# Nine weight blocks of the merge multiplied as seven products of quarters instead of eight

## The chip, the cores and the metric

One core of a Trainium2 chip runs the whole program. The metric is the time of one execution on the device in microseconds (us); the kernel before has a median of 2540.18 us over 3 runs (2537.29 to 2540.43). The core has a matrix engine (TensorE, PE in the profile, with its weight loads as PEld), a vector engine (DVE), a scalar engine (ACT), GpSimd (POOL) and a queue engine that issues transfers (SP). Each of them works off its own list of instructions in order, and waits on semaphores that the others raise.

## The reference, cut to what matters

Two transformer blocks run one after the other on 1024 tokens of width 1024, in float32. The place of the change is the input projection of the second block's mixer, and there the eight quarter-width outputs that gate it:

```
proj = xn @ w_in
qk, v, o, i_pre, f_pre, u, sv, gates = jnp.split(proj, SPLIT_POINTS, axis=-1)
h   = mlstm_chunkwise(q, k, v, i_pre + b_i, f_pre + b_f)
y_a = rmsnorm_2(h, mh_norm_g) * jax.nn.sigmoid(o)
y_b = jax.nn.gelu(u) * mixed            # spatial gating
g_a, g_b = jnp.split(jax.nn.sigmoid(gates + b_gate), 2, axis=-1)
return (g_a * y_a + g_b * y_b) @ w_out
```

So `xn` (1024 tokens by 1024) is multiplied with the columns of `u`, of `g_b`, of `o` and of `g_a`, 1024 columns each, and what comes out gates two results that are ready by then. After the mixer come the cross attention over a memory and a mixture of 32 experts.

## The kernel before, in words

**Numbers as two halves.** A float32 matrix goes to TensorE as two matrices in the engine's own 32-bit format: a rounded one (h, the high part, made by an ACT copy) and the rest (l, the low part, made by a DVE subtraction). The helper `split` (L230 and L231, or L233 and L234 with a scale) does this. A product of two such numbers is three matmuls: high by high, high by low, low by high.

**Weights as blocks.** The class `Stream` brings the weights in blocks of 256 columns: `load` (L88) has one 1 MB block brought into the tile `raw`, of which there is one only; `convert` splits it into `wh` and `wl` (four ACT copies and four DVE subtractions of 128x512); `next` hands a block out and starts the conversion of the one after it. The conversion is put on a list, `todo`, and `run` takes a step from it (and one from a second list, `bg`) at every other step of the main program. In the end a scheduler sets the order of the instructions on each engine, by its own estimates of their times.

**The merge.** `merge(gp, mp, p)` runs for p = 0 to 3, each for a quarter (256 columns) of u, b (g_b), o and g (g_a), so 16 blocks in all; they have the numbers 20 to 35 in the stream, and p = 1 to 3 has the blocks 24 to 35. The normalized tokens lie transposed in `hT` as four tiles: a high and a low one for tokens 0 to 511, and the same for tokens 512 to 1023. For each block there are four runs of `chan`, one for each half of the columns (j) and of the tokens (n): 8 steps of k (128 rows of the contraction) by 3 matmuls of 128x512 into one PSUM bank (L195). Behind each run, ACT applies gelu or tanh to the bank and writes the tile `e` (L1133, L1136, L1140), and DVE multiplies it into `mx_t` or `ya_t` (L1134, L1137, L1142; for g a second operation, L1144, adds both up). The PSUM has eight banks: two each with the tags m, b and c, and a pair with the tag a. The runs of the merge use the two m banks in turn.

**What lies around it.** The last head of the mLSTM runs beside merge 0 and its end reaches into the first block of merge 1; it stores its output (`ya_d<-yaT`, L1112), which merges 1 to 3 load through POOL's queue (L1121, L1122). Behind the merge the finished tile `mx_t` is split into `hT` again (L233, L234), the output projection `out_add` starts with products of 128x256 (`tok`, L206), and `mem_norm` loads the memory (`x<-in_mem`, L1186), squares it on ACT (L256), scales it on DVE (L1190) and transposes it on TensorE (L268) among those products.

Of the kernel before, what the change touches and what calls it, by code (L numbers as in the profile page):

```python
# [12 lines left out]
F32 = mybir.dt.float32  # L13
F32R = mybir.dt.float32r
I32 = mybir.dt.int32
AF = mybir.ActivationFunctionType
ALU = mybir.AluOpType
# [3 lines left out]
S = 1024  # L21
# [30 lines left out]
def f(ap):  # L52
    return ap.bitcast(F32)
# [19 lines left out]
class Stream:  # L73


    def __init__(self, prog, pool, seq):
        self.p, self.pool, self.seq = prog, pool, seq
        self.nraw = self.ncv = self.nuse = 0
        self.raw, self.cv = {}, {}
        self.slow = {}  # L80
        self.other = {}

    def load(self):
        if self.nraw < len(self.seq):
# [8 lines left out]

    def convert(self, pool=None):
        i = self.ncv
        if i >= len(self.seq):
            return
        while self.nraw <= i:
            self.load()
        r = self.raw.pop(i)  # L100
        n = r.shape[2]
        if isinstance(pool, tuple):
            h, l = pool
# [6 lines left out]
        m = max(1, 512 // n)  # L110
        for a in range(0, K, m):
            self.p.todo.append(lambda a=a: self.p.split(
                h[:, a:a + m], l[:, a:a + m], r[:, a:a + m],
                engine=self.p.nc.gpsimd if a // m in self.slow.get(i, ()) else None))
        self.p.todo.append(lambda: self.load() if self.nraw <= i + 1 or self.nraw - 1 in self.other else None)

    def next(self, pool=None):

# [10 lines left out]
class Prog:  # L129
# [22 lines left out]
    def two(self):  # L152
        return self.ps.tile([128, 1024], F32, tag="a", name="ps_a", bufs=1)
# [566 lines left out]
    def mixer(self):  # L720
# [27 lines left out]
                pass  # L748
        c2.close()
        c2 = ExitStack()  # L750
        mp = self.pool(c2, "mg2")
        for p in range(1, 4):
            self.run(self.merge(gp, mp, p))
        h, l = self.hT
# [360 lines left out]
    def merge(self, gp, mp, p2):  # L1115

        nc = self.nc
        mx = self.mg[p2] = gp.tile([128, 2, S], F32, tag="qqkk"[p2], name="mx_t")
        ya = mp.tile([128, 2, S], F32, tag="ya" if p2 else "k", name="ya_t")
        for j in range(2):  # L1120
            nc.gpsimd.dma_start(mx[:, j], self.mx_d[2 * p2 + j])  # L1121
            nc.gpsimd.dma_start(ya[:, j], self.ya_d[2 * p2 + j])  # L1122
        for what in "ubog":
            w = self.ws.next()
            for j in range(2):
                g = 2 * p2 + j
                for n in (0, 512):
                    ns = slice(n, n + 512)
                    p = self.bank()
                    yield from self.chan(p, w, j, self.hT, n)  # L1130
                    e = gp.tile([128, 512], F32, name="e")
                    if what == "u":
                        nc.scalar.activation(e, p, AF.Gelu_apprx_tanh)  # L1133
                        nc.vector.tensor_tensor(mx[:, j, ns], e, mx[:, j, ns], op=ALU.mult)  # L1134
                    elif what == "o":
                        nc.scalar.activation(e, p, AF.Tanh, scale=0.5)  # L1136
                        nc.vector.scalar_tensor_tensor(ya[:, j, ns], e, 1.0, ya[:, j, ns], op0=ALU.add, op1=ALU.mult)  # L1137
                    else:
                        o = 8 + g if what == "b" else g
                        nc.scalar.activation(e, p, AF.Tanh, scale=0.5, bias=self.hgate[:, o:o + 1])  # L1140
                        x = mx if what == "b" else ya
                        nc.vector.scalar_tensor_tensor(x[:, j, ns], e, 1.0, x[:, j, ns], op0=ALU.add, op1=ALU.mult)  # L1142
                        if what == "g":
                            nc.vector.scalar_tensor_tensor(mx[:, j, ns], ya[:, j, ns], 0.5, mx[:, j, ns],  # L1144
                                                           op0=ALU.mult, op1=ALU.add)

# [896 lines left out]

WSEQ = [0, 1, 2, 3] + [4, 5, 6, 7] + [-1] + list(range(8, 55))
MEM0 = 40


COLS = {}  # L2050
# [102 lines left out]
```

## Time and profile before

| | before |
|---|---|
| median of 3 runs | 2540.18 us (2537.29 to 2540.43) |
| the profiled execution | 2540.5 us, span 2538.9 us |
| PE busy | 2464.8 us (97% of the span) |
| DVE busy | 1587.4 us (63%) |
| ACT busy | 1331.1 us (52%) |
| granted TensorE clock, mean | 0.99 of full speed |

The span is what the profiler sees of the program; 1.6 us of the profiled execution lie around it. A busy share is the time in which an engine had at least one instruction under way; the matmuls are pipelined, so the start of one and the start of the next tell more than the length of one. The profile's chain of waits follows the end of the program back from one releaser to the next; it stays in the experts, where PE is busy without a pause. Rows of the timeline give the start in us from the span's start, the length in us, the engine, the line, what is written and read, and in square brackets the idle time of the engine just before and what ended it.

### The profile page before, as it was taken

The numbers are of one execution on the slowest core, as the hardware profiler recorded it, in microseconds if no ns is written. First come the engines' busy times: TensorE is split into PE (matmuls) and PEld (weight loads), VectorE is DVE, ScalarE is ACT, GpSimd is POOL, SyncE is SP. The second block draws the span as 40 slices with busy tenths as digits, with TensorE's granted clock in tenths as the row PEclk, the third lists the DMA queues.
The fourth block names the chain that finished last, engine by engine and source line by source line (L and its number), as shares of the span: only waits on it lengthen the run. The fifth ranks groups of instructions, "written<-read, shape, count | busy, mean of one in ns | idle before, by whom it ended". The sixth has DMA issues, their size and how long they took to land. (4 is left out here: it accounts for less than half of the span.)

```text
span 2538.9 us, 37146 instructions
## 1 busy us (share of the span) xinstructions
PE 2464.8 (97%) x14412; PEld 2141.9 (84%) x14412; DVE 1587.4 (63%) x2918; ACT 1331.1 (52%) x2318; POOL 310.0 (12%) x403
## 2 busy tenths in 40 slices
PE   7999999999999999999999999999989999999995
PEld 7978888889998988888888899888977888888884
DVE  6358676676345778755222265435368999997896
ACT  4257676673433544533222243334227888887885
POOL 3212121001100000000000000000122121111112
PEclk9999999999999999999999999999989999999998
DMA  6455453333221112112221133202468998998995
GB/s 216 131 147 161 136 155 100 95 117 134 76 99 61 50 42 75 67 59 88 95 92 50 67 134 117 100 29 96 164 232 313 364 361 322 386 381 313 345 359 204
DMA packets 72133, 414.50 MB, mean 163 GB/s; under 512 B 13607, under 2 KB 13767, under 8 KB 52624
## 3 DMA queue, kind: packets, MB, share of 16 engines
q1 hardware_dynamic: 42560, 315.22, 34.7%
q0 software_dynamic: 29392, 96.87, 11.6%
q8 instruction: 114, 1.87, 0.3%
q14 instruction: 67, 0.55, 0.1%
HBM read 361.51 MB, written 68.70 MB: 169 GB/s over the span
## 5 line engine op out<-in xcount | busy, mean ns | idle before, releaser
L195 PE MATMUL ps_m<-hT,wh 128*128 128x512 f32 x2624 | 838.2, 400 | 0.0
L231 DVE TENSOR_TENSOR wl<-raw,wh 128x1024 fp32r<-128x1024 f32 (+2 forms) x666 | 641.2, 994 | 221.0 <-ACT wh L230 219.3
L230 ACT ACTIVATE wh<-raw 128x1024 fp32r<-128x1024 f32 (+2 forms) x672 | 562.5, 869 | 194.4 <-PE ps_m L195 90.3
L195 PEld LDWEIGHTS ps_m<-hT,wh 128*128 128x128 f32 x2624 | 466.4, 189 | 78.5
L206 PE MATMUL ps_m<-wh,hT 128*128 128x256 f32 (+1 forms) x2816 | 525.7, 282 | 4.3 <-DVE ifg L893 1.1
L195 PE MATMUL ps_m<-hT,wl 128*128 128x512 f32 x1312 | 517.4, 394 | 0.0
L206 PEld LDWEIGHTS ps_m<-wh,hT 128*128 128x128 f32 x2816 | 440.6, 188 | 5.9 <-DVE y L705 1.5
L206 PE MATMUL ps_m<-wl,hT 128*128 128x256 f32 (+1 forms) x1408 | 394.8, 280 | 1.0 <-DVE wl L231 0.7
L195 PEld LDWEIGHTS ps_m<-hT,wl 128*128 128x128 f32 x1312 | 246.5, 188 | 55.9
L206 PEld LDWEIGHTS ps_m<-wl,hT 128*128 128x128 f32 x1408 | 265.3, 188 | 1.6 <-DVE wl L231 0.9
L2008 PE MATMUL ps_m<-wh,xgT_h 128*128 128x512 f32 x512 | 207.0, 404 | 1.3 <-ACT xgT_h L1958 1.3
L2008 PE MATMUL ps_m<-wh,xgT_l 128*128 128x512 f32 x512 | 202.8, 396 | 1.7 <-DVE xgT_l L1960 1.7
L2008 PE MATMUL ps_m<-wl,xgT_h 128*128 128x512 f32 x512 | 201.5, 394 | 0.0
L245 POOL TENSOR_TENSOR rs_y<-rs_a,mhalf 128x1 f32<-128x1 f32 (+2 forms) x58 | 39.2, 676 | 637.0 <-DVE rs_a L244 634.1
L2008 PEld LDWEIGHTS ps_m<-wh,xgT_l 128*128 128x128 f32 x512 | 96.4, 188 | 24.1 <-DVE xgT_l L1960 2.6
L2008 PEld LDWEIGHTS ps_m<-wh,xgT_h 128*128 128x128 f32 x512 | 96.6, 189 | 20.5 <-ACT xgT_h L1958 1.9
L2008 PEld LDWEIGHTS ps_m<-wl,xgT_h 128*128 128x128 f32 x512 | 96.7, 189 | 20.1
L2008 PE MATMUL ps_c<-wh,ht_h 128*128 128x512 f32 x256 | 101.4, 396 | 2.3 <-ACT ht_h L230 1.5
L2008 PE MATMUL ps_c<-wl,ht_h 128*128 128x512 f32 x256 | 101.6, 397 | 0.7 <-DVE wl L231 0.7
L2008 PE MATMUL ps_c<-wh,ht_l 128*128 128x512 f32 x256 | 101.8, 398 | 0.0
L532 ACT ACTIVATE P<-P,mx 128x128 f32<-128x128 f32 (+3 forms) x96 | 74.4, 775 | 44.5 <-DVE mx L530 41.2
L231 DVE TENSOR_TENSOR pl<-ps_b,ph 128x512 fp32r<-128x512 f32 (+1 forms) x120 | 75.1, 633 | 26.4 <-ACT ph L230 25.7
(532 smaller groups left out, 3636.5 us busy)
## 6 DMA issues: line engine op xcount, KB each, us to landing
raw<-in_w SPq DMA_DIRECT2D x85, 2048.0 KB, 13.1
raw<-in_wpack SPq DMA_DIRECT2D x55, 1024.0 KB, 4.9
raw<-in_w POOLq DMA_DIRECT2D x7, 2048.0 KB, 9.6
raw<-in_w_z SPq DMA_DIRECT2D x26, 512.0 KB, 4.0
kS<-k_d SPq DMA_DIRECT2D x48, 256.0 KB, 5.7
x<-in_x SPq DMA_DIRECT2D x16, 512.0 KB, 4.0
v_d<-vs POOLq DMA_DIRECT2D x24, 256.0 KB, 3.6
vS<-v_d SPq DMA_DIRECT2D x12, 512.0 KB, 3.3
```

Source lines behind the costliest of these rows:

```text
L195: nc.tensor.matmul(ps, lhsT=a[:, k, cs], rhs=b[:, k, n0:n0 + m], start=(k == 0 and a is wh and b is xh), stop=(k == K - 1 and a is wl))
L206: nc.tensor.matmul(ps, lhsT=a[:, k, ts], rhs=b[:, k, :], start=(k == 0 and a is xh and b is wh), stop=(k == K - 1 and a is xl))
L230: pin(nc.scalar.activation(h, src, AF.Copy))
L231: pin((engine or nc.vector).tensor_tensor(l, src, f(h), op=ALU.subtract))
L245: pin(nc.gpsimd.tensor_tensor(y, a, self.mhalf[:, :n], op=ALU.pow))
L532: nc.scalar.activation(e[:, :L], e[:, :L], AF.Exp, bias=mx[:, 0:1], scale=-1.0, accum_out=mx[:, 1:2])
L2008: pin(nc.tensor.matmul(z.ps, lhsT=a[:, k0 + k], rhs=b[:, k if self.which is None else 0], start=first and not k and not j, stop=last and k ...
```

## The change

Blocks 27 to 35 (`QUARTERS` = 27 to MEM0 - 4 = 36, nine blocks: g of merge 1, and all of merges 2 and 3) are no longer multiplied by four runs of `chan`. The block of weights is cut into quarters a(n, k): 128 of its 256 columns by 512 of its 1024 rows. The tokens are cut into quarters b[k][m]: 512 of the 1024 rows by 512 of the 1024 tokens. The product of such two-by-two matrices takes eight products of quarters; Strassen's scheme, in the form with the fewest sums, takes seven products of sums of quarters, and sums of the results.

- `quarters` makes the sums of the tokens once, in the list `bg` during blocks 24 to 26: three sums split into high and low (`t1` to `t3`, three tiles of 16 KB in each partition, in the pool of the merge), and a fourth (`t4`) that is split, in `late`, over a quarter of `hT` that no product needs any more. `self.tq` is the list of the seven right-hand sides.
- `Stream.piece(i, j)` makes the left-hand side of product j of block i: a quarter as it is (j = 0, 2, 5), or a sum of quarters (s, d), split into a tile `wp`. These tiles take turns in the memory of `wh` and `wl`, eight in all. The last piece of a block starts the load of the next block.
- `seven` is a block: ahead of each of its seven products it asks for a piece of the next block, then come 4 steps of k by 3 matmuls of 128x512, and then the sums of results. Two results of four are accumulated in PSUM; for the others ACT copies the first bank to `u` and DVE adds banks to it. The four gates, now the function `gate`, come behind products 2, 4, 5 and 6, three of them from a tile in SBUF and not from a bank. It uses one m bank for products 0 and 2, b for 1, c for 4 and 6, and the other m bank for 3 and 5.
- The tile `ya` of merges 1 to 3 now has one buffer, not two.

```diff
@@ -93,7 +94,7 @@
 
     def convert(self, pool=None):
         i = self.ncv
-        if i >= len(self.seq):
+        if i >= len(self.seq) or i in self.quarters:
             return
         while self.nraw <= i:
             self.load()
...
@@ -113,6 +114,37 @@
+    def piece(self, i, j):
+        nc = self.p.nc
+        while self.nraw <= i:
+            self.load()
+        r = self.raw[i]
+        TT = nc.vector.tensor_tensor
+        def a(n, k):
+            return r[:, 4 * k:4 * k + 4, 128 * n:128 * n + 128]
+        x = self.pool.tile([128, 2, 4, 128], F32R, tag=("wh", "wl")[self.npiece % 2], name="wp", bufs=4)
+        self.npiece += 1
+        h, l = x[:, 0], x[:, 1]
+        if j == 1:
+            self.s = [self.room.tile([128, 4, 128], F32, name="s") for _ in range(2)]
+            TT(self.s[0], a(1, 0), a(1, 1), op=ALU.add)
+            TT(self.s[1], self.s[0], a(0, 0), op=ALU.subtract)
+        elif j in (3, 6):
+            d = self.room2.tile([128, 512], F32, tag="e", name="d").rearrange("p (k n) -> p k n", k=4)
+            TT(d, a(0, j == 6), a(1, 0) if j == 3 else self.s[1], op=ALU.subtract)
+        src = {0: lambda: a(0, 0), 1: lambda: self.s[1], 2: lambda: a(0, 1), 4: lambda: self.s[0],
+               5: lambda: a(1, 1)}.get(j, lambda: d)()
+        self.p.split(h, l, src)
+        if j == 6:
+            self.raw.pop(i)
+            self.ncv = i + 1
+            if self.nraw <= i + 1:
+                self.load()
+        return h, l
...
@@ -748,7 +780,10 @@
                 pass
         c2.close()
         c2 = ExitStack()
-        mp = self.pool(c2, "mg2")
+        mp = self.ws.room = self.pool(c2, "mg2")
+        self.ws.room2 = gp
+        self.ws.quarters = range(QUARTERS, MEM0 - 4)
+        self.quarters(gp, mp)
         for p in range(1, 4):
             self.run(self.merge(gp, mp, p))
@@ -1116,33 +1151,147 @@
-        ya = mp.tile([128, 2, S], F32, tag="ya" if p2 else "k", name="ya_t")
+        ya = (mp.tile([128, 2, S], F32, name="ya", bufs=1) if p2 else gp.tile([128, 2, S], F32, tag="k", name="ya_t"))
...
+        ws = self.ws
         for what in "ubog":
-            w = self.ws.next()
+            if ws.nuse in ws.quarters:
+                yield from self.seven(gp, mp, lambda *x, what=what: gate(what, *x))
+                continue
+            w = ws.next()
+            if ws.nuse in ws.quarters:
+                self.pieces = []
+                self.todo += [lambda: None] * 9
+                self.todo += [lambda j=j, i=ws.nuse: self.piece(i, j) for j in range(4)]
             for j in range(2):
-                g = 2 * p2 + j
                 for n in (0, 512):
...
                     p = self.bank()
                     yield from self.chan(p, w, j, self.hT, n)
...
+                    gate(what, j, n, p)
+    def quarters(self, gp, mp):
+        nc = self.nc
+        TT = nc.vector.tensor_tensor
+        h, l = self.hT
+        b = [[tuple(x.tiles[m][:, 4 * k:4 * k + 4] for x in (h, l)) for m in range(2)] for k in range(2)]
+        t = [mp.tile([128, 2, 4, 512], F32R, name=f"t{j}", bufs=1) for j in range(3)]
+        t4 = gp.tile([128, 2, S], F32, tag="k", name="t4").rearrange("p a (b n) -> p (a b) n", b=2)
+        t1, t2, t3 = ((x[:, 0], x[:, 1]) for x in t)
+        self.tq = [b[0][0], t2, b[1][0], t3, t1, b[0][1], b[1][1]]
+        f1, f2, f3 = {}, {}, {}
+        def whole(o, x, k):
+            TT(o, f(x[0][:, k]), f(x[1][:, k]), op=ALU.add)
+        def part(o, src, k):
+            self.split(o[0][:, k], o[1][:, k], src)
+        def one(k):
+            f1[k] = mp.tile([128, 512], F32, tag="u", name="f1")
+            f2[k], f3[k] = (mp.tile([128, 512], F32, tag="s", name="f") for _ in range(2))
+            whole(f2[k], b[0][1], k)
+            whole(f1[k], b[0][0], k)
+        def two(k):
+            TT(f1[k], f2[k], f1[k], op=ALU.subtract)
+            part(t1, f1[k], k)
+        def three(k):
+            whole(f3[k], b[1][1], k)
+            TT(f2[k], f3[k], f2[k], op=ALU.subtract)
+            part(t3, f2[k], k)
+        def four(k):
+            TT(f3[k], f3[k], f1[k], op=ALU.subtract)
+            part(t2, f3[k], k)
+        def five(k):
+            whole(t4[:, k], b[1][0], k)
+            TT(t4[:, k], t4[:, k], f3[k], op=ALU.subtract)
+        for k in range(4):
+            for go in (one, two, three, four, five):
+                self.bg += [lambda go=go, k=k: go(k), lambda: None]
+        self.late = [lambda k=k: part(b[0][1], t4[:, k], k) for k in range(4)]
+    def piece(self, i, j):
+        self.flush_bg()
+        self.pieces.append(self.ws.piece(i, j))
+    def seven(self, gp, mp, done):
+        nc, ws = self.nc, self.ws
+        TT = nc.vector.tensor_tensor
+        i = ws.nuse
+        self.flush()
+        self.flush_bg()
+        pieces, ahead = self.pieces, []
+        b1, b2, b3, b4 = (self.bank(x) for x in "mbcm")
+        order = b1, b2, b1, b4, b3, b4, b3
+        for j in range(7):
+            while len(pieces) < 7 and not j:
+                pieces.append(ws.piece(i, len(pieces)))
+            if i + 1 in ws.quarters:
+                ahead.append(ws.piece(i + 1, j))
+            elif j == 4:
+                ws.convert()
+            if self.late:
+                self.late.pop(0)()
+            ps, (wh, wl), (xh, xl) = order[j], pieces[j], self.tq[j]
+            for k in range(4):
+                for n, (a, b) in enumerate(((wh, xh), (wh, xl), (wl, xh))):
+                    nc.tensor.matmul(ps, lhsT=a[:, k], rhs=b[:, k], start=(j in (0, 1, 3, 4) and not k and not n),
+                                     stop=(j in (1, 2, 5, 6) and k == 3 and n == 2), skip_group_check=True)
+                yield
+            if j == 0:
+                u = mp.tile([128, 512], F32, name="u")
+                nc.scalar.activation(u, b1, AF.Copy)
+            elif j == 1:
+                TT(u, u, b2, op=ALU.add)
+            elif j == 2:
+                done(0, 0, b1)
+            elif j == 3:
+                e = gp.tile([128, 512], F32, name="e")
+                TT(e, u, b4, op=ALU.add)
+            elif j == 4:
+                TT(e, e, b3, op=ALU.add)
+                done(1, 512, e, e)
+            elif j == 5:
+                e = gp.tile([128, 512], F32, name="e")
+                TT(e, u, b4, op=ALU.add)
+                done(1, 0, e, e)
+            else:
+                TT(u, u, b3, op=ALU.add)
+                done(0, 512, u, u)
+        ws.nuse += 1
+        self.pieces = ahead
@@ -2045,6 +2194,7 @@
 
 WSEQ = [0, 1, 2, 3] + [4, 5, 6, 7] + [-1] + list(range(8, 55))
 MEM0 = 40
+QUARTERS = 27
```

In the rows of the order below, `wh`, `wl` and `wp` are split weights, `raw` is the loaded block, `e` the gate's tile, `u` the copied first bank, `s` and `d` are sums of weight quarters, and `t_12777`, `t_12778` and `t_12779` are t1, t2 and t3, the right-hand sides of the products 4, 1 and 3. A semaphore named DMAHW stands for a transfer of SP's queue, DMASW for one of POOL's. The rows of after are from block 28 (u of merge 2) for ACT and DVE and from block 29 for PE, those of before from merge 3.

PE before, from the end of one run of `chan` into the next:

```order
L195 MATMUL ps_m<-hT,wl 128x512
L195 MATMUL ps_m<-hT,wh 128x512 [waits Activation_49]
L195 MATMUL ps_m<-hT,wh 128x512
L195 MATMUL ps_m<-hT,wl 128x512
L195 MATMUL ps_m<-hT,wh 128x512 x2
```

and PE after, one whole block, seven products of twelve matmuls:

```order
L1270 MATMUL ps_m<-hT,wp 128x512 [waits Activation_49]
L1270 MATMUL ps_m<-hT,wp 128x512 x11
L1270 MATMUL ps_b<-t_12778,wp 128x512 x12
L1270 MATMUL ps_m<-hT,wp 128x512 [waits Activation_49]
L1270 MATMUL ps_m<-hT,wp 128x512 x11
L1270 MATMUL ps_m<-t_12779,wp 128x512 [waits DVE_49]
L1270 MATMUL ps_m<-t_12779,wp 128x512 x11
L1270 MATMUL ps_c<-t_12777,wp 128x512 x12
L1270 MATMUL ps_m<-hT,wp 128x512 [waits DVE_49]
L1270 MATMUL ps_m<-hT,wp 128x512 x11
L1270 MATMUL ps_c<-hT,wp 128x512 [waits DVE_49]
L1270 MATMUL ps_c<-hT,wp 128x512 x11
```

Before has one wait at the head of each run of 24 matmuls, for ACT to have emptied the bank; after has five waits in a block of 84, for ACT at the products 0 and 2, and for DVE at the products 3, 5 and 6.

ACT before, from the conversion of one block (the next) to the gates of another:

```order
L230 ACTIVATE wh<-raw 128x512 [waits DMAHW6_49,PE_49]
L230 ACTIVATE wh<-raw 128x512
L230 ACTIVATE wh<-raw 128x512 [waits PE_49]
L1140 ACTIVATE e<-ps_m,hgate 128x512 [waits DVE_49,PE_49]
L230 ACTIVATE wh<-raw 128x512
L1136 ACTIVATE e<-ps_m 128x512 [waits DVE_49,PE_49] x3
```

and ACT after, one block:

```order
L1275 ACTIVATE u<-ps_m 128x512 [waits PE_49]
L262 ACTIVATE wp<-raw 128x512 [waits DMAHW0_49]
L262 ACTIVATE wp<-raw 128x512 [waits PE_49]
L262 ACTIVATE wp<-s 128x512 [waits DVE_49]
L1164 ACTIVATE e<-ps_m 128x512 [waits PE_49,Activation_49]
L262 ACTIVATE wp<-d 128x512 [waits DVE_49]
L262 ACTIVATE wp<-s 128x512 [waits PE_49]
L262 ACTIVATE wp<-raw 128x512 [waits PE_49]
L1164 ACTIVATE e<-e 128x512 [waits DVE_49,Activation_49] x2
L262 ACTIVATE wp<-d 128x512 [waits DVE_49,PE_49]
L1164 ACTIVATE u<-u 128x512 [waits DVE_49]
```

ACT's copy of the first bank, `u<-ps_m`, stands ahead of the first piece, which waits for the load; the eight instructions of a block (four copies, four gates) have become twelve, and some of them now wait for DVE.

DVE before, over the end of one block and the start of the next:

```order
L1137 SCALAR_TENSOR_TENSOR ya_t<-e,ya_t 128x512 [waits DMASW2_49,Activation_49]
L231 TENSOR_TENSOR wl<-raw,wh 128x512 [waits DMAHW7_49,PE_49,Activation_49]
L231 TENSOR_TENSOR wl<-raw,wh 128x512 [waits Activation_49]
L231 TENSOR_TENSOR wl<-raw,wh 128x512 [waits DVE_49,PE_49,Activation_49]
L1137 SCALAR_TENSOR_TENSOR ya_t<-e,ya_t 128x512 [waits Activation_49]
L231 TENSOR_TENSOR wl<-raw,wh 128x512 [waits Activation_49]
L1142 SCALAR_TENSOR_TENSOR ya_t<-e,ya_t 128x512 [waits Activation_49]
L1144 SCALAR_TENSOR_TENSOR mx_t<-ya_t,mx_t 128x512 [waits DVE_49]
```

and DVE after, from the first use of a loaded block to the sum of results that product 6 waits for:

```order
L134 TENSOR_TENSOR s<-raw 128x512 [waits DMAHW0_49]
L263 TENSOR_TENSOR wp<-raw,wp 128x512 [waits Activation_49]
L135 TENSOR_TENSOR s<-s,raw 128x512 [waits DVE_49]
L1277 TENSOR_TENSOR u<-u,ps_b 128x512 [waits PE_49]
L263 TENSOR_TENSOR wp<-raw,wp 128x512 [waits Activation_49]
L263 TENSOR_TENSOR wp<-s,wp 128x512 [waits Activation_49]
L138 TENSOR_TENSOR d<-raw 128x512
L1165 TENSOR_TENSOR mx_t<-e,mx_t 128x512 [waits DMASW7_49,Activation_49]
L263 TENSOR_TENSOR wp<-d,wp 128x512 [waits PE_49,Activation_49]
L1282 TENSOR_TENSOR e<-u,ps_m 128x512 [waits DVE_49,PE_49]
L263 TENSOR_TENSOR wp<-s,wp 128x512 [waits Activation_49]
L1284 TENSOR_TENSOR e<-e,ps_c 128x512 [waits DVE_49,PE_49]
```

The sum `s` of the freshly loaded block now stands ahead of the sums of results of the running block.

## Rows read from the trace of the kernel before

**Rows 1.** The page's share of each engine over the whole span.

```profile
PE 2464.8 (97%) x14412; PEld 2141.9 (84%) x14412; DVE 1587.4 (63%) x2918; ACT 1331.1 (52%) x2318; POOL 310.0 (12%) x403
```

**Rows 2.** Stretches of the merge: start:end, length, busy time (instructions), PEclk, DMA.

```profile
1248.00:1275.00 27.00, 27.00 (x118) 21.94 (x118) 6.24 (x10) 5.35 (x10) 0.00 (x0) 1.00 0.23 76
1302.00:1329.00 27.00, 27.00 (x119) 21.95 (x118) 5.96 (x9) 5.36 (x9) 0.00 (x0) 1.00 0.21 80
```

**Rows 3.** Timeline of ACT: gates of the first run of block 25 and third of 35.

```profile
1230.01 0.69 ACT L1140 ACTIVATE e<-ps_m,hgate 128x512 f32<-128x512 f32 x1 [4.14 <-PE ps_m L195]
...
1463.03 0.69 ACT L1140 ACTIVATE e<-ps_m,hgate 128x512 f32<-128x512 f32 x1
```

**Rows 4.** Groups of instructions from 1225 to 1468 us: busy, mean ns, idle before.

```profile
L231 DVE TENSOR_TENSOR wl<-raw,wh 128x512 fp32r<-128x512 f32 x42 | 28.1, 688 | 33.3 <-ACT wh L230 33.3
L230 ACT ACTIVATE wh<-raw 128x512 fp32r<-128x512 f32 x41 | 24.7, 624 | 35.2 <-PE ps_m L195 35.2
L1140 ACT ACTIVATE e<-ps_m,hgate 128x512 f32<-128x512 f32 x23 | 15.7, 684 | 78.4 <-PE ps_m L195 78.3
```

**Rows 5.** The page's group of DVE subtractions that read PSUM.

```profile
L231 DVE TENSOR_TENSOR pl<-ps_b,ph 128x512 fp32r<-128x512 f32 (+1 forms) x120 | 75.1, 633 | 26.4 <-ACT ph L230 25.7
```

**Rows 6.** Timeline of DVE: two operations in a row, first independent, then dependent.

```profile
1201.14 0.69 DVE L1142 SCALAR_TENSOR_TENSOR ya_t<-e,ya_t 128x512 f32<-128x512 f32 x1
1201.75 0.69 DVE L231 TENSOR_TENSOR wl<-raw,wh 128x512 fp32r<-128x512 f32 x1
...
1275.10 0.69 DVE L1142 SCALAR_TENSOR_TENSOR ya_t<-e,ya_t 128x512 f32<-128x512 f32 x1 [3.94 <-ACT e L1140]
1275.83 0.69 DVE L1144 SCALAR_TENSOR_TENSOR mx_t<-ya_t,mx_t 128x512 f32<-128x512 f32 x1
```

**Rows 7.** Loads of weight blocks on SP from 1180 to 1500 us.

```profile
L88 SPq DMA_DIRECT2D raw<-in_wpack x17: 327/328/372, 1202.5 to 1497.8; - x17
...
DMA to landing us min/median/max: 4.7/4.8/6.8
```

**Rows 8.** Timeline of POOL around the end of the mLSTM and the merge.

```profile
1214.89 0.55 POOL L1112 DMA_DIRECT2D ya_d<-yaT  x1 [2.91 <-ACT yaT L1111]
...
1295.29 1.06 POOL L1186 DMA_DIRECT2D x<-in_mem  x2
```

**Rows 9.** Transfers from 1180 to 1500 us: KB each, median us to landing.

```profile
ya_d<-yaT POOLq DMA_DIRECT2D x2, 256.0 KB, 2.4
x<-in_mem POOLq DMA_DIRECT2D x2, 512.0 KB, 8.6
```

**Rows 10.** Timeline of all engines, from the merge's last matmuls on.

```profile
1468.08 0.40 PE L195 MATMUL ps_m<-hT,wl 128*128 128x512 f32 x1
...
1468.32 0.28 PE L206 MATMUL ps_m<-wh,hT 128*128 128x256 f32 x1
1468.44 0.28 PE L206 MATMUL ps_m<-wl,hT 128*128 128x256 f32 x1
...
1474.58 1.02 ACT L256 ACTIVATE ps_a<-x 128x1024 f32<-128x1024 f32 x1
...
1479.64 0.30 PE L268 MATMUL ps_b<-ident,x 128*128 128x128 f32 x1 [0.74 <-DVE x L1190]
```

**Rows 11.** Waits of PE from 1195 to 1500 us: us, times, longest.

```profile
PE ps_b L268 <- DVE x L1190: 0.7, 1, 0.7
```

**Rows 12.** A stretch of the experts, columns as in rows 2.

```profile
2200.00:2300.00 100.00, 100.00 (x474) 82.37 (x473) 92.11 (x89) 84.35 (x99) 14.16 (x11) 1.00 1.00 379
```

**Rows 13.** Waits of SP's queue over the whole span.

```profile
SPq L1687 <- DVE wl L231: 474.1, 81, 11.7
```

More of the change, by code (lines that the diff above doesn't have):

```diff
@@ L81, in __init__ @@
         self.other = {}
+        self.quarters, self.npiece, self.room, self.room2 = (), 0, None, None
     def load(self):
@@ L1122, in merge, with gate @@
             nc.gpsimd.dma_start(ya[:, j], self.ya_d[2 * p2 + j])
-        for what in "ubog":
-            w = self.ws.next()
+        def gate(what, j, n, p, e=None):
+            g, ns = 2 * p2 + j, slice(n, n + 512)
+            if e is None:
+                e = gp.tile([128, 512], F32, name="e")
+            if what == "u":
+                nc.scalar.activation(e, p, AF.Gelu_apprx_tanh)
+                nc.vector.tensor_tensor(mx[:, j, ns], e, mx[:, j, ns], op=ALU.mult)
+            elif what == "o":
+                nc.scalar.activation(e, p, AF.Tanh, scale=0.5)
+                nc.vector.scalar_tensor_tensor(ya[:, j, ns], e, 1.0, ya[:, j, ns], op0=ALU.add, op1=ALU.mult)
+            else:
+                o = 8 + g if what == "b" else g
+                nc.scalar.activation(e, p, AF.Tanh, scale=0.5, bias=self.hgate[:, o:o + 1])
+                x = mx if what == "b" else ya
+                nc.vector.scalar_tensor_tensor(x[:, j, ns], e, 1.0, x[:, j, ns], op0=ALU.add, op1=ALU.mult)
+                if what == "g":
+                    nc.vector.scalar_tensor_tensor(mx[:, j, ns], ya[:, j, ns], 0.5, mx[:, j, ns],
+                                                   op0=ALU.mult, op1=ALU.add)
@@ L1127, in merge @@
                 for n in (0, 512):
-                    ns = slice(n, n + 512)
                     p = self.bank()
                     yield from self.chan(p, w, j, self.hT, n)
[L1131 to L1145, printed above, removed]
@@ new lines, in piece @@
+    def piece(self, i, j):
[39 more added lines that the diff above has]
+            elif j == 5:
+                e = gp.tile([128, 512], F32, name="e")
+                TT(e, u, b4, op=ALU.add)
+                done(1, 0, e, e)
+            else:
+                TT(u, u, b3, op=ALU.add)
+                done(0, 512, u, u)
+        ws.nuse += 1
+        self.pieces = ahead
```

## Prediction

> **What bounds the kernel now.** I read the shares of the engines first: PE is busy 97% of the span, DVE 63%, ACT 52% [rows 1]. A share is an average, so I cut out the merge, where the change is. There PE is busy in 27.00 of 27 us at a granted clock of 1.00 (the 2.4 GHz level), while DVE is busy for 6.0 to 6.2 us and ACT for 5.4 us [rows 2]. The waits of PE from 1195 to 1500 us are one single wait of 0.7 us, behind the merge [rows 11]. So in this stretch nothing but the number of matmuls and the distance from one to the next sets the time, and two engines stand idle three quarters of it. Matmuls overlap in the trace, so their length is not their price; I take the price from ACT's gates, which follow each run of 24 matmuls: the gate of the first run of block 25 starts at 1230.01 and that of the third run of block 35 at 1463.03 [rows 3]. Between them lie 10 x 4 + 2 = 42 runs: 233.02 / 42 = 5.548 us a run, 0.2312 us a matmul, 22.19 us a block.
>
> **Part 1, the matmuls.** A block had 4 x 8 x 3 = 96 matmuls of 128x512 and has 7 x 4 x 3 = 84 of the same shape. Nine blocks: 108 fewer, 108 x 0.2312 = 25.0 us. A product takes 2.77 us, a block 19.42 us. A block has five waits where it had four; a wait that is met early costs nothing, as the one at the head of each old run shows (42 runs in a row at the same distance).
>
> The Trainium skill (TensorE: Matmul & The Clock Gate, Back-to-back issue gap) puts the warm distance of single matmuls at N / 2.4 + 2.5 ns, 216 ns here; an estimate by it would be 108 x 0.216 = 23.3 us saved. The trace disagrees, 231 ns with a weight load for each matmul, and the measurement decides.
>
> **Part 2, a steady block on DVE and ACT.** DVE had 4 subtractions and 4 gate operations (8 in g). It gets 7 subtractions, 4 sums of weights, 5 sums of results and 4 or 8 gate operations: 20, or 24 in g. ACT had 8 and gets 7 + 1 + 4 = 12. At 0.69 us for DVE and 0.62 to 0.68 us for ACT [rows 4] that is 13.8 (g: 16.6) and 7.8 us in 19.42 us. A DVE operation that reads PSUM is not shown in the merge; elsewhere it takes 0.63 us [rows 5], so 0.69 is the upper end; started one behind the other they come every 0.61 us when independent and 0.73 us when dependent [rows 6]. I use 0.69.
>
> It fits, but PE waits for these engines inside a block, so I follow the order from the block's start S. Product j ends at S + 2.77 (j+1), and its result is there some 0.16 us later (the last matmul starts at 1468.08 and is 0.40 long, the next starts at 1468.32 [rows 10]).
> - Product 2 goes on in the bank that ACT copies to `u`: the copy runs from S + 2.9 to 3.6, and product 2 starts at S + 5.55. Behind the copy on ACT, not ahead of it, stands the piece that waits for the load.
> - The load of the next block's weights can start when `raw` has been read for the last time, by the sum `d` of the block before. That stands behind the sum that waits for product 5: 16.8, then 0.69 twice, 18.2. A load lands 4.8 us after its issue [rows 7]: 23.0 of the old block, S + 3.6 of the new one.
> - DVE then does s, l, s (to 5.7), the sum for product 1 (6.4), l, l, d (8.5), the gate behind result 2 and ACT (8.5 + 0.68, so 9.2 to 9.9), l (10.6), and the sum `e` behind result 3 (11.3), to 12.0. Product 5, which overwrites that bank, starts at S + 13.87: 1.9 us to spare. In g one gate operation more still ends at 12.0.
> - The sum behind result 4 (14.0) ends at 14.7; product 6 starts at 16.64: 1.9 us to spare.
>
> With the longest landing of the rows, 6.8 us, the third point moves to 12.6 (g 13.3) and still holds. So I take 0 for the steady blocks; the other end is in the rivals.
>
> **Part 3, the sums of the tokens.** 44 DVE operations and 12 ACT copies, then 4 and 4 for `late`: 48 x 0.69 = 33 us of DVE and 10 us of ACT, once. All but the four first sums of t4 wait for memory that the mLSTM's last store frees: issued at 1214.89 [rows 8], landed 2.4 us later [rows 9], 1217.3. Block 25 starts at 1230.01 - 5.55 = 1224.5, block 26 ends at 1268.8. In these 51.5 us DVE has 40 sums, 10 gates, 4 subtractions of block 26 and 7 operations for the first pieces of block 27: 61 x 0.69 = 42 us, and the first product needs the last of them only at 1268.8. In block 27 it has 24 + 4 of `late` + 4 of the pieces that are still missing = 32, 22.1 us against 19.42; but the order has most of the 8 in the last run of block 26, whose readers let go of the memory step by step. Cost between 0 and 2.7 us (22.1 - 19.4); I take 0.5, near the end at which they lie under that run.
>
> **Part 4, behind the merge.** Call the end of block 35 E (1468.32 before [rows 10]).
> - The output projection needs all of the tokens 0 to 127. The last of them come from the gate of product 5, whose second half stands on DVE behind the sum of product 6: E + 0.16 + 0.69 + 0.69 = 1.5; ACT's split 2.2; DVE's split 2.9, or 4.3 with two operations ahead. The projection reaches it after 21 matmuls of 0.12 us [rows 10], at E + 2.5. Cost 0 to 1.8 us; I take 0.5, since the scheduler has put other matmuls in between.
> - `x<-in_mem` was issued at 1295 [rows 8]. It now lies in memory that a sum of the tokens holds, t2 by the sizes, so it waits for product 1 of block 35: E - 13.9 + 1.1 + 8.6 [rows 8, 9] = E - 4.2, and ACT squares it at E + 6.3 [rows 10]. Cost 0; if it waits for the block's end, E + 9.7, 3.4 us. The 0.7 us that PE waited there may also go.
> - POOL's other transfers for the merge (mx, ya with one buffer) are issued a block or more ahead of their gates: 0.
>
> Everything later moves as it is: in the experts PE is busy 100 of 100 us [rows 12].
>
> **The sum.** -25.0 + 0.5 + 0.5 = -24.0 us. The profiled execution, 2540.5 us (span 2538.9 and 1.6 around it), becomes 2516.5; the median lies 0.3 lower: 2516.2 us. Its own range: 25.0 + 0.7 saved and half the 3.1 us spread of the runs below, 2513; 2.2, 1.3 and 3.4 us of the bounds above, 2523.
>
> **Rivals.**
> - *A, DVE's hand-overs.* DVE waits for ACT in 7 places of a block (three sums that ACT must round before DVE subtracts, four gates). If nothing lies under these waits: 20 x 0.69 + 7 x 0.65 = 18.4, still under 19.42; but g takes 24 x 0.69 + 4.6 = 21.1, 1.7 over, in three blocks, and block 27 has 4 x 0.69 more: 7.9 us, 2524 us. For it: strict order on each engine. Against: the order has independent work in most of these places.
> - *B, slower: ACT and DVE take strict turns.* One `raw` only, and DVE's first sum of a new block, which waits for its load, stands ahead of the sums of results that PE waits for. If each ACT instruction is waited for, a block takes 20 x 0.69 + 12 x 0.65 = 21.6 (g 24.4), 2.2 and 4.9 us over: 6 x 2.2 + 3 x 4.9 + 4 x 1.34 for block 27 = 33 us against 25 saved, 2549 us. It decides from the point where DVE is more than 1.9 us late in every block. Against: four of the seven pieces are taken from `raw` without a sum, so ACT can run ahead.
> - *C, given back in the experts.* There the DMA engines are busy at 1.00 with 379 GB/s [rows 12]; if the weights set the pace, an earlier start is lost: 2540 us. Against: SP waits 474 us for DVE to free `raw` before these loads [rows 13], so the loads follow the work.
> - *D, the memory's load is late* (part 4): 3.4 us, 2519.6 us.
> - That fewer matmuls are not what is built is ruled out by the order: seven times twelve.
>
> **How the numbers follow.** Forecast 0.72, D 0.08, A 0.13, C 0.04, B 0.03. A measurement of this kernel tells some 0.2% (5 us) from no change. Faster by more: forecast, D and A, 0.93; the same: C, 0.04; slower: B, 0.03. The range 2513 to 2523 holds the forecast, D and part of A, a bit over 0.8.
>
> **What would show it.** Right: matmuls of the seven 0.231 us apart and blocks of 19.4 us, no wait of PE on `u` or `e`, DVE at 70 to 85% there, the output projection about 24 us earlier. Wrong: PE waiting at products 5 or 6 for DVE in each block (A, B), at the transposes of the memory (D), or a shift that is gone by the end (C). A matmul distance other than 0.231 us would make part 1 wrong.

## The result, and the profile after

The changed kernel takes 2513.18 us, the median of 4 runs (2512.12 to 2515.04), beside 2538.73 us of the kernel before in the same comparison: 25.55 us less, ratio 0.990 with a 95% interval of 0.9888 to 0.9913. Forecast were 2516.2 us and a range of 2513.0 to 2523.0, a gain of 24.0 us. Compared twice more, it gained 24.1 and 23.7 us. In the first comparison of the experiments three of the 23 executions of the kernel before were slow (3044 to 4940 us): its median of 2540.45 us counts them, without them it is 2539.75, and the ratios leave them out. The profiled execution went from 2540.5 to 2514.0 us (span 2538.9 to 2512.4).

The page's shares, to be read beside [rows 1]:

```profile
PE 2442.9 (97%) x14304; PEld 2123.6 (85%) x14304; DVE 1686.1 (67%) x3074; ACT 1363.4 (54%) x2370; POOL 310.8 (12%) x403
```

PE has 108 instructions and 21.9 us less; DVE has 156 more, ACT 52 more. So DVE took on 99 us of busy time, and the kernel still became 25 us shorter: the share of busy time says nothing until one sees beside what the work lies. Windows of the merge (start:end, length, then busy time and instructions of PE, PEld, DVE, ACT, POOL, then PEclk, the DMA share and GB/s), beside [rows 2]; the first, in which the sums of the tokens are made, has no fellow there:

```profile
1220.00:1248.00 28.00, 28.00 (x123) 22.77 (x122) 27.96 (x47) 13.72 (x24) 0.00 (x0) 1.00 0.16 58
1302.00:1329.00 27.00, 27.00 (x118) 21.86 (x117) 18.43 (x28) 10.25 (x17) 0.00 (x0) 1.00 0.16 52
```

PE stays busy throughout, 27.00 of 27 us among the blocks. DVE is full for 28 us while the sums of the tokens are made, and is at 18.43 of 27 us (68%) among the blocks. The list of PE's waits from 1195 to 1500 us is empty: the one of [rows 11] is gone and none has come.

The timeline of PE shows block 30, from 1327.79, seven products of twelve matmuls each, and the end of the merge (start, length, and how many matmuls the row holds); it answers to [rows 3, 10]:

```profile
1325.03 2.92 PE L1270 MATMUL ps_c<-hT,wp 128*128 128x512 f32 x12
1327.79 2.91 PE L1270 MATMUL ps_m<-hT,wp 128*128 128x512 f32 x12
1330.54 2.96 PE L1270 MATMUL ps_b<-t,wp 128*128 128x512 f32 x12
1333.34 2.96 PE L1270 MATMUL ps_m<-hT,wp 128*128 128x512 f32 x12
1336.14 2.96 PE L1270 MATMUL ps_m<-t,wp 128*128 128x512 f32 x12
1338.94 2.96 PE L1270 MATMUL ps_c<-t,wp 128*128 128x512 f32 x12
1341.74 2.95 PE L1270 MATMUL ps_m<-hT,wp 128*128 128x512 f32 x12
1344.53 2.96 PE L1270 MATMUL ps_c<-hT,wp 128*128 128x512 f32 x12
1347.33 2.92 PE L1270 MATMUL ps_m<-hT,wp 128*128 128x512 f32 x12
...
1444.84 0.28 PE L238 MATMUL ps_m<-wh,hT 128*128 128x256 f32 x1
```

The block takes 1347.33 - 1327.79 = 19.54 us; 19.42 were forecast. The merge ends at 1444.84, 23.5 us earlier than the 1468.32 of [rows 10].

Starts and ends differ by some 3 us between executions of one program, as will be seen, so I use a yardstick inside the merge: from ACT's gate behind the second run of block 26, which is a plain block in both kernels, to the first matmul of the output projection. Before, the gate stands five runs of 5.548 us behind the 1230.01 of [rows 3], at 1257.75, and the yardstick is 1468.32 - 1257.75 = 210.57 us. After, by the timeline of ACT:

```profile
1258.29 0.60 ACT L1167 ACTIVATE e<-ps_m 128x512 f32<-128x512 f32 x1 [4.89 <-PE ps_m L227]
```

1444.84 - 1258.29 = 186.55 us, so 24.02 us less for nine blocks, 2.67 a block. Two later profiles of the changed kernel give 186.54 and 186.65.

### The profile page after: what moved, and what is told of

It reads as the page before. It is cut to its first block, busy times and chain, and to the rows that moved or that the text cites. A ratio compares the mean times of both kernels' runs of the same rounds, so it can differ in the third digit from the quotient of the medians.

```text
span 2512.4 us, 37138 instructions
## 1 busy us (share of the span) xinstructions
PE 2442.9 (97%) x14304; PEld 2123.6 (85%) x14304; DVE 1686.1 (67%) x3074; ACT 1363.4 (54%) x2370; POOL 310.8 (12%) x403
## 5 line engine op out<-in xcount | busy, mean ns | idle before, releaser
L263 DVE TENSOR_TENSOR wl<-raw,wh 128x1024 fp32r<-128x1024 f32 (+1 forms) x630 | 617.3, 1012 | 187.1 <-ACT wh L262 185.4
L227 PE MATMUL ps_m<-hT,wh 128*128 128x512 f32 x2048 | 658.9, 402 | 0.0
L262 ACT ACTIVATE wh<-raw 128x1024 fp32r<-128x1024 f32 (+2 forms) x636 | 540.5, 882 | 153.1 <-PE ps_m L227 51.5
L227 PEld LDWEIGHTS ps_m<-hT,wh 128*128 128x128 f32 x2048 | 358.3, 189 | 54.3
L227 PE MATMUL ps_m<-hT,wl 128*128 128x512 f32 x1024 | 404.0, 395 | 0.0
L227 PEld LDWEIGHTS ps_m<-hT,wl 128*128 128x128 f32 x1024 | 192.4, 188 | 43.1
L263 DVE TENSOR_TENSOR pl<-ps_b,ph 128x512 fp32r<-128x512 f32 (+1 forms) x120 | 75.2, 634 | 26.5 <-ACT ph L262 25.9
```

What stands on the lines that cost most here:

```text
L227: nc.tensor.matmul(ps, lhsT=a[:, k, cs], rhs=b[:, k, n0:n0 + m], start=(k == 0 and a is wh and b is xh), stop=(k == K - 1 and a is wl))
L262: pin(nc.scalar.activation(h, src, AF.Copy))
L263: pin((engine or nc.vector).tensor_tensor(l, src, f(h), op=ALU.subtract))
```

## The experiments

I had three readings. The first: the gain is the matmuls of nine blocks and nothing else, and all that the scheme adds lies beside them. The second: a part of the gain is a fixed one, from the memory's load that has moved, or from the stages behind. The third: DVE's work costs something, which the matmuls pay for.

**Only the fixed part.** The sums of the tokens, the new places of `ya` and the load stay; no block is done in seven products.

```
-QUARTERS = 27
+QUARTERS = 36
```

> No block is done in seven products (36 in place of 27); the sums of the tokens and the new places of ya and of the memory's load stay. Before is 2538.7 us, the changed kernel 2513.2. Theory 1 (the gain is the matmuls of nine blocks): the sums of the tokens lie under the matmuls and what is left costs 0 to 0.6 us (block 27 started 0.6 us later than before in the trace), so 2538.0 to 2539.5 us. Theory 2 (a part of the gain is a fixed one, from the memory's load that now lands in time and from the stages behind): 2536 to 2537.5 us, so 1.5 to 3 us under before with no matmul less. Theory 3 (the sums cost time that the matmuls pay for): over 2540 us.

Measured: 2540.65 us beside 2540.45 (ratio 1.0, 0.9991 to 1.0009). The expected times were set beside 2538.7 us, so it is the difference that counts, and the ratio shows none. In its profile the gate stands at 1258.67 and the output projection begins at 1469.25, which is 210.58 us, as before. But this yardstick begins behind the sums of the tokens, so it can't tell what they cost. A mark ahead of them is the transposes of the mLSTM's output (eight matmuls in one row); the first row is of the kernel before, the next two are of this run, the last is of the changed kernel:

```profile
1207.25 1.20 PE L1108 MATMUL ps_b<-ident,hs 128*128 128x128 f32 x8
```
```profile
1208.18 1.20 PE L1143 MATMUL ps_b<-ident,hs 128*128 128x128 f32 x8
1469.25 0.28 PE L238 MATMUL ps_m<-wh,hT 128*128 128x256 f32 x1
```
```profile
1207.81 1.20 PE L1143 MATMUL ps_b<-ident,hs 128*128 128x128 f32 x8
```

Before, 1468.32 - 1207.25 = 261.07 us; here 1469.25 - 1208.18 = 261.07; changed 1444.84 - 1207.81 = 237.03, 24.04 less. The 28 us of DVE cost nothing, and the fixed part gains nothing. The second reading falls. The third falls for this part. PE's wait of 0.7 us at the transposes of the memory is there, though the load here is issued 84 us ahead of the merge's end:

```profile
1384.96 1.06 POOL L1335 DMA_DIRECT2D x<-in_mem  x2
...
1480.56 0.30 PE L300 MATMUL ps_b<-ident,x 128*128 128x128 f32 x1 [0.73 <-DVE x L1339]
```

So that wait was never one for the load. It is one for DVE's scaling of `x`, which starts at 1479.66, 10.4 us behind the merge's end. In the changed kernel the scaling is no earlier, 11.5 us behind the end (1456.30); there the wait is gone because the order on PE has the first transpose later, 12.8 us behind the end and not 11.3:

```profile
1457.68 0.27 PE L300 MATMUL ps_b<-ident,x 128*128 128x128 f32 x1
```

**All of the scheme's work with the old number of matmuls.** The first product of each block is multiplied twice into its bank; the second time starts the bank anew, so the result is the same, and the steps that the main program yields to DVE and ACT stay as many.

```
-            for k in range(4):
...
+            for twice in range(2 if j == 0 else 1):
+                for k in range(4):
...
+                    if not twice:
+                        yield
```

> The first product of each block is multiplied twice into the same bank, so that a block has 96 matmuls again, with all of the scheme's work on DVE and ACT. Theory 1 (matmul count alone): 108 x 0.2323 = 25.1 us more than the changed kernel, 2538.3 us, within 1 us of before. Theory 2 (a fixed gain of 1.5 to 3 us beside the count): 25.1 more as well, but below before by that gain only if the changed kernel's sum has it: 2536 to 2537.5. Theory 3 (DVE's and ACT's work holds PE up inside the blocks): a product more hides what held it, and the difference to the changed kernel is under 23 us.

Measured: 2540.21 us beside 2540.45 (ratio 1.0003, 0.9993 to 1.0012). By the yardstick 1469.16 - 1258.63 = 210.53 us. With 96 matmuls a block the kernel is the one before again, though DVE and ACT do all that the scheme asks. Take the 108 matmuls away and 24.0 us go. This pair is the proof of the first reading. It alone does not rule out a hold-up by DVE, since a longer block would hide one; the changed kernel's own list of waits, which is empty, does.

**Five blocks and ten blocks.** One number each, 31 and 26 in place of 27.

> Five blocks in seven products in place of nine (31 in place of 27). A block took 19.52 us in the changed kernel's trace against 22.19, 2.67 less. Theory 1 (the gain goes with the blocks and passes through zero): five ninths of 25.5, 14.2 us, so 2524.5 us (4 x 2.67 = 10.7 over the changed kernel gives 2523.9). Theory 2 (a fixed gain beside it): also 2523.9, with the run without any such block below before by what is left. Theory 3 (a fixed cost, a larger gain for each block): more than 2525.5 us. With the run without such blocks and the one with ten it gives the slope of a block.

> Ten blocks in place of nine (26 in place of 27): one block more saves 2.67 us. In the changed kernel's trace DVE is busy without a gap from 1217.3, when the last store has freed the memory, to the last of the sums at 1247.6, and block 26 starts at 1246.9 and wants its second product's tokens at 1249.7, and its seven pieces of weights besides. Theory 1 (the sums bound where the scheme can begin): the pieces of block 26, 7 to 9 operations at 0.60, come on top, so PE waits 2 to 6 us at the head of block 26 and the time is 2513 to 2517 us, no gain. Rival (DVE's order puts the sums that are needed first ahead, the rest under the first products): PE doesn't wait and the time is 2510.5 us.

Five blocks: 2526.84 us beside 2540.45 (ratio 0.9945, 0.9932 to 0.9958). The yardstick is 1455.99 - 1258.78 = 197.21 us, 13.36 less than 210.57, 2.67 a block, to the hundredth the slope of nine. So nothing fixed stands beside the slope. Ten blocks: 2510.30 us beside 2540.45 (0.9888, 0.9873 to 0.9903). Here I was wrong with what I held likelier, a wait of 2 to 6 us at the head of block 26. DVE's order mixes the sums and the first pieces closely enough; all of PE's waits in the merge are

```profile
PE ps_m L1270 <- DVE e L1282: 0.8, 1, 0.8
```

**Eleven blocks.** 25 in place of 27, to find where the start of the sums decides.

> Eleven blocks in place of nine (25 in place of 27). Theory 1 (the sums of the tokens, which begin at 1217.3 to 1218.5 when the last store has landed, bound the start): 40 of them at 0.60 us with some 10 other operations end at about 1248; block 25 begins at 1224.5 and wants the first of its second product's tokens at 1227.3, so PE waits 15 to 20 us there; against ten blocks (2510.3) one block saves 2.7 and the 0.8 us wait goes: 2523 to 2527 us. Rival (the matmuls follow the sums closely enough): 2507.6 us.

Measured: 2528.19 us beside 2539.81 (0.9953, 0.9939 to 0.9966), 18 us more than ten blocks took in the other comparison. The timeline of PE at the head of the scheme (in brackets: idle time before, and whom PE waited for):

```profile
1225.66 2.92 PE L1270 MATMUL ps_m<-hT,wp 128*128 128x512 f32 x12
1233.57 5.49 PE L1270 MATMUL ps_m<-hT,wp 128*128 128x512 f32 x12 [4.98 <-ACT u L1275]
1241.51 0.73 PE L1270 MATMUL ps_c<-t,wp 128*128 128x512 f32 x2 [2.45 <-ACT wp L262]
1242.71 4.74 PE L1270 MATMUL ps_b<-t,wp 128*128 128x512 f32 x12 [0.47 <-ACT wp L262]
1247.29 2.96 PE L1270 MATMUL ps_m<-t,wp 128*128 128x512 f32 x12
```

and windows of it:

```profile
1218.00:1226.00 8.00, 8.00 (x36) 6.47 (x35) 8.00 (x14) 3.70 (x6) 0.00 (x0) 1.00 0.12 47
1228.60:1233.50 4.90, 0.00 (x0) 0.00 (x0) 4.90 (x10) 2.36 (x4) 0.00 (x0) 0.89 0.00 0
1234.00:1239.00 5.00, 5.00 (x12) 3.38 (x11) 5.00 (x10) 2.08 (x4) 0.00 (x0) 0.50 0.00 0
```

DVE is busy without a gap in these windows, nearly all of it with the tokens' sums: they are the bound. PE's own waits name other things. ACT's copy `u`, its first wait, stands in ACT's list behind splits that wait for these sums, and the pieces `wp`, its other two, are made from sums of weights that stand behind them on DVE. PE does what needs none of the tokens' sums (the third product ahead of the second) and waits 7.9 us, half of what I had expected. The waits are not the whole price. After 5 us without work the granted clock is 0.50, the 1.2 GHz level, and a row of twelve matmuls takes 5.49 us where the row before the wait took 2.92; the twelve from 1242.71 take 4.74. From 1225.66 to 1247.29 PE runs 38 matmuls, 8.8 us at 0.231; it takes 21.6, so 12.8 are lost, 7.9 to waits and the other 4.9 in the main to the clock (2.6 and 1.8 in these two rows). Less the 2.7 of a block that makes 10.1 us, and by so much the merge ends later than with ten blocks, at 1453.02 and 1442.90. The profiled spans differ by 15.7: 10.1 at the merge's end and 5.6 behind it, of which 3.2 are a wait that will be met below; the other 2.4 no row explains. The medians differ by 18, but ten blocks' second median, below, is 2.6 over its first. So the bound is shown, its price in the merge is 10 us, and that the median came out 1.2 over the 2523 to 2527 expected is chance: half the waits, with a price for the clock and the end of the program that I had not counted.

**The slack in front of product 5.** The sum `e` that frees product 5's bank is made three, then seven times.

```
-                TT(e, u, b4, op=ALU.add)
+                for _ in range(7):
+                    TT(e, u, b4, op=ALU.add)
```

> In each block of the scheme the sum for product 5's bank, e = u + product 3's result, is made three times in place of once, so that the bank comes free two DVE operations later. In the changed kernel's trace that sum of block 28 runs from S + 11.4 to S + 12.1 and product 5 starts at S + 14.0: 1.9 us to spare. Theory 1 (the slack is what the order leaves, 1.9 us): 2 x 0.60 to 0.69 = 1.2 to 1.4 us later, still early, 2513 us as without. Rival A (DVE's hand-overs already sit near the edge): each block some 0.5 us longer, 4 to 6 us, 2518.

> The same sum made seven times: six DVE operations more, 3.6 to 4.1 us, in front of product 5. DVE would have 14.2 + 3.8 = 18 of 19.5 us to do, so by its share it still fits. Theory 1 (the place in the order decides, not the share): the bank is free 3.6 - 1.9 = 1.7 to 2.2 us too late in each of nine blocks, PE waits there, 15 to 20 us in all: 2528 to 2533 us. Rival (only the share counts): 2513 to 2516 us.

Three times: 2514.77 us, beside 2515.70 of the changed kernel in the same comparison; no cost. It is no clean measure of the 1.9 us, though, since the order on PE moved with it. PE waits once, at the head of block 27; in block 28 the last of the three sums ends at 1302.89, and the row from 1302.81, of thirteen matmuls, begins with one of the next block, which fills the time until then:

```profile
PE ps_m L1270 <- DVE e L1283: 1.0, 1, 1.0
```
```profile
1302.81 3.16 PE L1270 MATMUL ps_m<-hT,wp 128*128 128x512 f32 x13
```

So two more sums use up the slack, and the order finds a matmul to hide it. Seven times: 2525.02 us, 9.3 more. That lies between the two theories (15 to 20 us, and 0 to 3). The waits of PE from 1268 to 1462 us with seven:

```profile
PE ps_m L238 <- ACT wh L262: 1.3, 1, 1.3
PE ps_m L1270 <- DVE e L1283: 1.1, 2, 0.6
PE ps_m L1270 <- ACT wp L262: 1.0, 3, 0.4
PE ps_c L1270 <- ACT wp L262: 0.9, 3, 0.3
PE ps_m L238 <- DVE wl L263: 0.9, 1, 0.9
PE ps_m L238 <- DVE hT L266: 0.3, 1, 0.3
```

and windows of the end of the merge:

```profile
1440.00:1450.00 10.00, 7.80 (x34) 6.24 (x34) 9.96 (x17) 4.75 (x9) 0.53 (x1) 0.86 0.48 157
1450.00:1460.00 10.00, 9.40 (x55) 8.19 (x54) 9.08 (x16) 6.57 (x11) 0.00 (x0) 0.97 0.57 211
```

For `e` itself PE waits only 1.1 us in all. The scheduler, which sees the sums, put products of the next block ahead of product 5, here of block 27:

```profile
1281.14 2.92 PE L1270 MATMUL ps_c<-t,wp 128*128 128x512 f32 x12
1283.89 2.96 PE L1270 MATMUL ps_m<-hT,wp 128*128 128x512 f32 x12
1286.68 1.99 PE L1270 MATMUL ps_b<-t,wp 128*128 128x512 f32 x8
1289.17 3.02 PE L1270 MATMUL ps_m<-hT,wp 128*128 128x512 f32 x12 [0.49 <-DVE e L1283]
```

The fifth product (`ps_c<-t`) is followed by the next block's first and eight matmuls of its second (`ps_b<-t`), and only then by the sixth. So here too the order on PE changed, and more. What it shows: DVE's lateness can be pushed along from block to block while there is a next block, and more than half of the waiting is done at the last one: of the 5.5 us that PE is idle (the rows' sum), 2.5 are waits of the output projection and 0.6 one for the last `e`, and the clock drops to 0.86 there. The rest are waits of 0.3 to 0.5 us in the blocks ahead. How the remaining 4 us of the 9.3 divide between the clock and the order, I leave open.

**The same programs again.** Three kernels in one comparison, unchanged.

> The kernel before, profiled a second time. From the end of the merge to the end of the span its first profile took 1070.6 us with one wait of 6.4 us of PE's own sequencer, the changed kernel's 1067.6 with the same wait at 2.9. Theory 1 (that wait is a matter of the execution, not of the change): the wait can come out at 3 us here too and the rest at 1067 to 1068; the end of the merge stands at 1468.3 plus or minus 0.5. Rival (the change shortens it): 6.2 to 6.4 us again and 1070 to 1071.

> The changed kernel again, to stand beside ten blocks in one comparison. 25 us under before. In its first profile two of eight pieces' buffers gave matmuls 0.229 us apart and the other six 0.233, in its second four of eight, with the same program. Theory 1 (the distance belongs to the execution): one of the two patterns again, block 19.4 or 19.5 us. Rival (it belongs to the program): the same pattern as in the last one, whatever the chip.

> Ten blocks again beside nine. Theory 1 (one block's 2.7 us less 0.2 to 0.8 us of wait for DVE in the first block): 1.9 to 2.7 us under nine, 27 us under before. Rival (the wait in the first block eats it): as nine.

Before: 2539.29 us, with 2539.22 beside it. Nine blocks 2515.54 (0.9908, 0.9891 to 0.9924), ten blocks 2512.87 (0.9892, 0.9876 to 0.9909): 2.67 us less, what a block is worth. The intervals overlap, so by times alone ten and nine are not told apart. From the transposes of the mLSTM's output to the output projection the two profiles of ten blocks take 1442.90 - 1208.50 = 234.40 and 1445.84 - 1211.24 = 234.60 us, the three of nine 237.03, 237.03 and 237.14: 2.4 to 2.7 us less each time. So I take ten as the better version, and it beats both kernels.

The second profile of before has the yardstick at 1471.42 - 1260.85 = 210.57 us, as the first. But its gate stands 3.1 us later than the first profile's, and behind the merge it is 4.4 us shorter (2537.6 - 1471.42 = 1066.2, beside 1070.6). Of that, 3.4 us are one wait of PE's own sequencer, 6.4 us in the first profile and in the second

```profile
PE ps_m L215 <- PEq L1748: 3.0, 1, 3.0
```

The changed kernel had 2.9 us there, and with eleven blocks it was 6.2. It belongs to the execution and not to the change.

## Why the prediction was right

The starts on which parts 1 and 2 rest are those of the first product of all, of block 28, and of its products 5 and 6 (counted from 0):

```profile
1269.19 2.91 PE L1270 MATMUL ps_m<-hT,wp 128*128 128x512 f32 x12
...
1288.74 2.96 PE L1270 MATMUL ps_m<-hT,wp 128*128 128x512 f32 x12
...
1302.73 2.92 PE L1270 MATMUL ps_m<-hT,wp 128*128 128x512 f32 x12
1305.49 2.91 PE L1270 MATMUL ps_c<-hT,wp 128*128 128x512 f32 x12
```

**Part 1, the matmuls: right.** Forecast -25.0 us at 0.2312 us a matmul. The 63 products take 1444.84 - 1269.19 = 175.65 us from the first one on, 0.2323 a matmul, so what was taken from nine old blocks is 9 x 22.19 - 175.65 = 24.1. The missing 0.9 us is the distance, 1.1 ns more for each of 756 matmuls. That size isn't even a property of the program: in another profile of the same kernel the distance is 0.231 and the block 19.4 us (below); there PE waited 0.7 us at the head, and the yardstick came out the same.

**Part 2, the steady blocks at 0: right, and step by step.** Block 28 starts at S = 1288.74. DVE's timeline from there:

```profile
1300.13 0.69 DVE L1282 TENSOR_TENSOR e<-u,ps_m 128x512 f32<-128x512 f32 x1 [0.80 <-PE ps_m L1270]
...
1302.93 0.69 DVE L1284 TENSOR_TENSOR e<-e,ps_c 128x512 f32<-128x512 f32 x1 [1.44 <-PE ps_c L1270]
...
1306.30 0.69 DVE L138 TENSOR_TENSOR d<-raw,s 128x512 f32<-128x512 f32 x1
...
1311.85 0.69 DVE L134 TENSOR_TENSOR s<-raw 128x512 f32<-128x512 f32 x1 [1.33 <-DMA raw<-in_wpack]
```

The sum `e` ends at S + 12.1 (forecast 12.0) and product 5 starts at 1302.73, S + 14.0: 1.9 us to spare, as forecast. The sum before product 6 ends at 1303.62, product 6 starts at 1305.49: 1.9 again. The last read of `raw` ends at S + 18.2, as forecast, and the load has landed at 1311.85, 3.6 us into the next block, the forecast to the tenth. Taking 0.69 us for every DVE operation was a little too much: operations that stand one behind the other start 0.60 to 0.67 us apart in this timeline. So DVE is at 68% among these blocks where I wrote 70 to 85; in g of merge 2 it is busy 14.22 of 19.50 us, 73%.

**Part 3, the sums of the tokens: right, with an end too high.** Cost forecast 0 to 2.7, taken 0.5; the fixed part alone costs 0.0 from the mark ahead of the sums, and the head of block 27 costs 0.1 us in this execution (product 5 and its follower start 2.86 us apart, not 2.80) and 0.7 in another.

**Part 4, behind the merge: 0 where 0.5 was taken.** No wait of PE on the output projection. DVE's split of what product 5's gate finishes ended 3.9 us behind the merge's end (1448.76), between the two ends of the forecast, 2.9 and 4.3, and later than the 2.5 at which it could be wanted; that nothing waited bears out the reason given, other matmuls in between. `x<-in_mem` is issued at 1431.4, E - 13.4 (forecast E - 13.9), and lands 4.2 us later, not 8.6. The wait of 0.7 us went, but not for the load, with which the prediction put it: the order on PE had changed, as the fixed part showed. That this came out was luck.

**The sum.** In the yardstick -24.0 us, where parts 1 and 3 gave -24.5. The profiled spans differ by 26.5: the gate stands 0.5 later, the merge gives 24.0, and 3.0 come behind the merge, where the sequencer's wait of 6.4 or 3 us accounts for 3.5. The three comparisons give 25.6, 24.1 and 23.7 us. The forecast of 24.0 lies among them, and I don't claim the 1.5 us that the first has over it for anything in the change. That it fits to a few tenths is partly luck: part 1 had 0.9 us too much, and the 0.5 and 0.5 taken for parts 3 and 4, of which 0.1 came, made up for it. Luck too is that 2513.18 us lies inside the range by 0.2 us; the two later medians, 2515.70 and 2515.54, lie well inside.

**The rivals.** A and B: no wait of PE inside a block; with two more DVE operations in each PE waited 1.0 us, once, at the head, and only with six more did the time grow. C: the merge ends 24.0 us earlier by the yardstick and the medians keep 23.7 to 25.6 of it. D: the load lands 16 us before ACT reads it at 1452.0. The mechanism of "DVE becomes the bound" is real all the same: eleven blocks put it where I had not looked, at the start of the scheme and not in its steady state.

## What to carry to other kernels

Where PE has no gap and another engine has three quarters of its time free, see whether work can be moved from the one to the other: here 99 us of DVE cost nothing and 108 matmuls came off. The price of a matmul is the distance to the next, taken over many runs, not its length in the trace. Before such a scheme is spread wider, ask when its preparation can begin at all: here ten blocks are better than nine, and eleven cost 10 us in the merge, because the operands' sums can't start before memory comes free, and PE went on at a granted clock of 0.50 after a wait of 5 us. A gain of one per cent is read best between two marks inside the stage, since the ends of a span move by 3 us from execution to execution.

## What I had not expected of the hardware

Matmuls of one shape at a granted clock of 1.00 come at two distances. In the rows shown with block 30 the two products from 1325.03 and 1327.79 take 2.76 and 2.75 us, 0.229 a matmul, the others 2.79 to 2.80, 0.233. The next such pair is the one at 1347.33 and 1350.09, eight products further, and so from block 28 to the end of the merge. The pieces of the weights take turns in eight buffers, a block has seven products; so the pace goes with the turn of the weights' buffers, not with the tokens or the bank. In the kernel that multiplies a product twice, both halves of the 24 matmuls run at one pace. But the place in that turn doesn't fix the pace: the first two products of block 27, from 1269.19, take 2.74 and 2.76 us, and the two that stand eight further on, from 1291.54, take 2.80 each. And it is not the program alone: another profile of the same kernel has four products in eight at 0.229.

```profile
1325.63 2.91 PE L1270 MATMUL ps_c<-hT,wp 128*128 128x512 f32 x12
1328.38 2.92 PE L1270 MATMUL ps_m<-hT,wp 128*128 128x512 f32 x12
1331.13 2.96 PE L1270 MATMUL ps_b<-t,wp 128*128 128x512 f32 x12
1333.93 2.96 PE L1270 MATMUL ps_m<-hT,wp 128*128 128x512 f32 x12
1336.73 2.91 PE L1270 MATMUL ps_m<-t,wp 128*128 128x512 f32 x12
1339.47 2.92 PE L1270 MATMUL ps_c<-t,wp 128*128 128x512 f32 x12
...
1347.82 2.91 PE L1270 MATMUL ps_m<-hT,wp 128*128 128x512 f32 x12
```

Two at 0.229, two at 0.233. Ten blocks were profiled twice as well, once with four products in eight at 0.229 and once with two. Those two come from different chips, but the chip alone doesn't decide: five blocks, profiled on the chip on which ten had four, had two. What decides stays open. It is worth 0.1 us a block, which is the size of the error in part 1. By the Trainium skill (TensorE: Matmul & The Clock Gate, Back-to-back issue gap) single matmuls of this width are 216 ns apart; no product of these timelines comes under 228.
